# A hybrid decoder layer on one core: second feed-forward product by seven block products, first product in 256-wide parts

## The chip, the cores and the metric

The kernel runs on one core of a Trainium2 chip. The metric is the device time of one execution in microseconds (us). The kernel before takes 1446.87 us (median of 3 runs, 1446.61 to 1447.17).

## The reference

One layer on 256 tokens of width 2048, all in float32: a mixer (gated delta net and RWKV7 beside each other), a cross attention to 256 memory tokens, and a feed-forward part. The change touches the last:

```
h = h + squared_relu_mlp(rmsnorm(h, ffn_norm_w), ffn_w1, ffn_w2)   # max(u @ w1, 0)**2 @ w2
return rmsnorm(h, final_norm_w)
# w1: 2048 x 8192, w2: 8192 x 2048, both float32 and read once
```

## The kernel before

Engines are named as in the profile: PE is TensorE, DVE VectorE, ACT ScalarE, POOL GpSimd, SP the engine whose queue issues most transfers. The array multiplies in float32r, a shorter format, so every float32 operand x is split in two parts: hi is x rounded to float32r (a cast, on ACT), lo is x minus hi (a subtraction, on DVE). A product of two split operands takes three passes: hi hi, hi lo and lo hi. This holds for all large products; the weights are split as they arrive (`weights`, L228).

Stages, in the order of time: low-rank parts, RWKV7, delta net, output projection, cross attention, and from 721.9 us on the feed-forward, which is half of the span. It has four chunks (`ch`), and each chunk does two things.

First product, `gemm_T` (L261), four calls of four blocks each, 64 blocks in all. A block gives 128 hidden columns, transposed: [128 hidden, 256 tokens]. It has 16 k tiles. The weights are the stationary operand, and the moving operand holds x_hi and x_lo of a k tile beside each other, 512 columns. For each k tile L272 multiplies w_lo with x_hi (256 columns), and L273 multiplies w_hi with both halves (512 columns), into the two halves of one PSUM bank. `relu2` (L1186) then adds the halves (ACT copy, DVE add), squares the positive part (DVE) and splits it for the second product (ACT cast, DVE subtraction).

Second product, `gemm` (L244), four calls a chunk, one for each 512 of the 2048 output columns: 16 k tiles, two halves of the tokens, three passes of 512 columns each (L254 to L256), 96 matmuls a call and 1536 in all. The result is scaled and added to h by DVE. The very last call is `gemm_rows` (L205), which finishes the first 128 tokens before the others. Then `final` (L1140) applies the last norm and writes the output.

A block of weights of 512 KB comes from HBM by SP's queue into one of five buffers (pool `wp`, tag raw) and is split in pieces of [128 x 512]; three buffers each hold whi and wlo. The eight PSUM banks are three with the tag g (large products), two each of s0 and s1, and one x. The order on each engine is not the program's: a list scheduler places the instructions by priorities and its own estimate of times, and weight loads and splits have a high priority (`tc.high_priority(3000)`). Each engine then runs its own list in order, and waits on semaphores.

Of the kernel before, what the change touches and what calls it, by code (L numbers as in the profile page):

```python
# [17 lines left out]
P = 128  # L18
D = 2048
# [21 lines left out]
def host_layout(inp):  # L41
# [32 lines left out]
    def col(v):  # L74
# [22 lines left out]
        "w1": blocks_T(a["ffn_w1"][0]), "w2": blocks(a["ffn_w2"][0]),  # L97
# [7 lines left out]
def body(ctx, tc, I, out, dbg=None, upto=99):  # L105
# [65 lines left out]
    # derived per-channel scalars  # L171
# [15 lines left out]
    def lhs_split(raws, wname, pool, tag):  # L187
        """raw^T (times the norm's weight) split in two float32r parts, four k tiles a tile, as they are asked for."""
# [16 lines left out]
    def gemm_rows(lhs, wblk, evac, kbs, his, los):  # L205
        """the same, the first 128 tokens before the others, from weights that all stay."""
        kbs, w = list(kbs), []
        for m in range(2):
            acc = bank("g")
            for i, kb in enumerate(kbs):  # L210
                if m == 0:
                    with tc.high_priority(3000):
                        raw = wp.tile([P, KB, NB], F32, tag="raw", name=nm("raw"))
                        nc.sync.dma_start(out=raw, in_=wblk[kb])
                        hi, lo = his(), los()
                        A.copy(hi, raw)
                        tt(lo, raw, hi.bitcast(F32), ALU.subtract)
                    w.append((hi, lo))
                hi, lo = w[i]
                for q in range(KB):  # L220
                    first, last = i == 0 and q == 0, i == len(kbs) - 1 and q == KB - 1
                    xh, xo = lhs(kb * KB + q, m)
                    T.matmul(acc, lhsT=xh, rhs=hi[:, q], start=first, stop=False)
                    T.matmul(acc, lhsT=xh, rhs=lo[:, q], start=False, stop=False)
                    T.matmul(acc, lhsT=xo, rhs=hi[:, q], start=False, stop=last)  # L225
            evac(m, acc)

    def weights(src, a, b, parts):  # L228
        """a block of weights [128, a, b] in two float32r parts."""
# [14 lines left out]
    def gemm(lhs, wblk, n, evac, kbs=None):  # L244
        """[256 tok, n] = lhs^T @ W: three float32r products stand for the float32 one."""
# [15 lines left out]
    def gemm_T(rhs, wblk, evac):  # L261
        """(x W)^T in four parts of 128 columns, [128 col, (W x_hi, W_hi x_lo)]; rhs(kt) is (x_hi, x_lo)^T, 512 wide."""
        for j in range(4):
            acc = bank("g")
            for b in range(2):
                w = weights(wblk[j, b], 8, P, 2)
                for k in range(8):
                    first, last = b == 0 and k == 0, b == 1 and k == 7
                    x = rhs(8 * b + k)
                    xf = x.rearrange("p a t -> p (a t)")  # L270
                    if not first:
                        T.matmul(acc[:, 0:S], lhsT=w[k][1], rhs=x[:, 0], start=False, stop=False)  # L272
                    T.matmul(acc, lhsT=w[k][0], rhs=xf, start=first, stop=last)  # L273
                    if first:
                        T.matmul(acc[:, 0:S], lhsT=w[k][1], rhs=x[:, 0], start=False, stop=False)
            evac(j, acc)
# [84 lines left out]
    # the clock of the array rises and the functions' table loads while the first operands are on their way  # L361
# [73 lines left out]
    # gates of the deltanet: [tok, chunk, head]  # L435
# [35 lines left out]
    inv = [0]  # L471

    def inverse(B, pool, pool2):
        """B is overwritten with the inverse of I + (its strictly upper part); what lies below its diagonal is zero.

        X12 = -X11 B12 X22 for blocks of 2 to 128, the larger ones on tiles of the array."""
# [11 lines left out]
        def quarters(t, n):  # L488
            """the quarters 11, 12, 22 of the diagonal blocks of 2n: [q, block, row, column]."""
# [94 lines left out]
    def rw_shift(pt, c0, names, blks):  # L584
        """columns c0.. of the projection [tok, col] to shifted [col, tok] tiles of two blocks."""
# [12 lines left out]
    def rw_unit(u, r, k, v):  # L598
# [59 lines left out]
        # bonus * v  # L658
# [8 lines left out]
        # scores  # L667
# [21 lines left out]
        # [tok, .] forms  # L689
# [57 lines left out]
        # group norm, bonus, gate  # L747
# [94 lines left out]
    def dn_unit(g, kq, v2):  # L842
# [6 lines left out]
        # norms per token: [tok, (k/q), chunk, head]  # L849
# [21 lines left out]
        # decays, scores  # L871
# [72 lines left out]
        # norm over the head, times silu(z)  # L944
# [90 lines left out]
    def tok_T(src, wname):  # L1035
        """transposes of src [tok, 2048] (times the norm's weight), split in two parts, four k tiles a step."""
# [77 lines left out]
    rf = rms(h, "rf")  # L1114
    tt(rf, rf, rf, ALU.mult)
    mix.close()
    fp = ctx.enter_context(tc.tile_pool(name="fp", bufs=5, reuse_waits="tile"))
    fw = fp.tile([P, D], F32, name="fw", bufs=1)
    A.dma_start(out=fw, in_=I["fnw"].to_broadcast([P, D]))
    part = small.tile([P, 2, 8], F32, tag="sk", name=nm("ssp"))  # L1120

    def low():
        for _ in range(2):
            t = da.tile([P, 2, KB, NB], F32R, tag="kq", bufs=2, name=nm("llo"))
            yield t[:, 0]
            yield t[:, 1]
        for _ in range(4):
            yield fp.tile([P, KB, NB], F32R, tag="llo", bufs=4, name=nm("llo"))

    def high():  # L1130
        for _ in range(4):
            t = lx.tile([P, 2, KB, NB], F32R, tag="lx", name=nm("lhi"))
            yield t[:, 0]
            yield t[:, 1]

    llo, lhi = low(), high()

    def final(m):
        ss = part[:, m, 7:8]
        stt(ss, part[:, m, 4:5], 1.0 / D, part[:, m, 6:7], ALU.mult, ALU.add)  # L1140
        ro = small.tile([P, 1], F32, tag="ro", name=nm("ro"))
        power(ro, ss, -0.5, 1)
        for q in range(4):
            d = h[:, m, q * NB:(q + 1) * NB]
            if q == 3:
                stt(d, d, ro, fw[:, q * NB:], ALU.mult, ALU.mult)
            elif q:
                act(d, d, AF.Copy, scale=ro)
            else:
                ts(d, d, ro, ALU.mult)  # L1150
            (A if q % 2 else nc.sync).dma_start(out=out[m * P:(m + 1) * P, q * NB:(q + 1) * NB], in_=d)

    def add_ffn(gcol):
        def f(m, p):
            d = h[:, m, gcol * NB:(gcol + 1) * NB]
            stt(d, p, rf[:, m:m + 1], d, ALU.mult, ALU.add)
        return f

    def last_h(gcol):
        def f(m, p):  # L1160
            sl = slice(gcol * NB, (gcol + 1) * NB)
            d = h[:, m, sl]
            stt(d, p, rf[:, m:m + 1], d, ALU.mult, ALU.add)
            rms_part(h, part, m, gcol)
            tt(d, d, fw[:, sl], ALU.mult)
        return f

    def last(m, p):
        """the last 512 columns in two halves, so that little is left to do once the second's sum of squares is there."""
        V.tensor_reduce(part[:, m, 5:6], part[:, m, 0:3], axis=AX.X, op=ALU.add)  # L1170
        ts(part[:, m, 5:6], part[:, m, 5:6], 1.0 / D, ALU.mult, EPS, ALU.add)
        for i in range(2):
            d = h[:, m, 3 * NB + i * S:3 * NB + (i + 1) * S]
# [51 lines left out]
```

## Time and profile before

| | |
|---|---|
| median of 3 runs | 1446.87 us |
| span of the profiled execution, first to last instruction | 1442.5 us |
| median less the span (start and end around it) | 4.4 us |
| feed-forward, 721.9 us to the last matmul | 712.5 us |
| last matmul to the end of the span | 8.1 us |
| PE, DVE, ACT busy over the span | 98%, 66%, 54% |

The page's parts give the busy time of each engine, the DMA engines over 40 slices of the span, the chain that ended last, and groups of equal instructions. A matmul row's length contains its way through the array; matmuls overlap, so the distance from one start to the next is what one costs, not its length. The same holds in a small way for DVE and ACT, where the next instruction starts a little before the end of the one ahead.

### The profile page before, as it was taken

The page shows a single profiled execution, that of the slowest core. Times are in us where ns is not written, and L with a number is a line of the kernel's source. Part 1 is how long each engine was busy: PE and PEld are TensorE (multiplying, and loading weights), DVE is VectorE, ACT ScalarE, POOL GpSimd, SP SyncE. Part 2 cuts the span into 40 slices and gives each one's busy share as a digit, 9 for nine tenths or more (in the row PEclk, how much of TensorE's full clock was granted, in tenths as well). Part 3 has the DMA queues.
Part 4 walks back from the last instruction along what each step waited for, and adds up shares of the span by engine and source line. Part 5 has one row for each costly group of instructions (what it writes and reads, how often), then busy time and mean ns, then how long its engine had stood idle before and what let it go on. Part 6 is the DMA issues. An engine that isn't in the chain of part 4 may idle for free.

```text
span 1442.5 us, 22496 instructions
## 1 busy us (share of the span) xinstructions
PE 1414.8 (98%) x8284; PEld 1168.9 (81%) x8284; DVE 950.1 (66%) x1799; ACT 780.8 (54%) x1491; POOL 50.6 (4%) x66
## 2 busy tenths in 40 slices
PE   9999999999999989999999999999999999999997
PEld 7877788787876868887788888888888888888886
DVE  7748574869587685767676655666556665566664
ACT  7656454555456454566565544555445554455553
POOL 0010001100010000000000000000000000000000
PEclk9999999999999999999999999999999999999999
DMA  7444433454366464556465556555665555655554
GB/s 281 157 145 152 135 121 112 147 177 144 102 200 207 138 190 146 166 173 212 136 209 186 190 192 197 185 187 189 193 197 186 185 190 194 195 182 187 191 188 146
DMA packets 90688, 252.88 MB, mean 175 GB/s; under 512 B 20673, under 2 KB 29393, under 8 KB 90193
## 3 DMA queue, kind: packets, MB, share of 16 engines
q1 hardware_dynamic: 70304, 243.96, 51.2%
q10 hardware_dynamic: 19920, 6.42, 1.8%
q8 instruction: 65, 1.06, 0.3%
q0 software_dynamic: 352, 1.06, 0.2%
q14 instruction: 47, 0.38, 0.1%
HBM read 244.72 MB, written 6.69 MB: 174 GB/s over the span
## 4 chain that ended last, share of the span: by engine, by line
PE 82%; DMA 7%; DVE 6%; ACT 3%; issue 2%; SPq 0%; POOL 0%; ACTq 0%; POOLq 0%; DVEq 0%
PE ps_g L273 16%; PE ps_g L255 16%; PE ps_g L254 15%; PE ps_g L256 15%; PE ps_g L272 8%; DVE wlo L110 2%; PE ps_s L675 2%; DMA scr<-Sc 1%; DMA xc<-inv 1%; DMA mraw<-in_memT_dram 1%; PE ps_x L312 1%; DMA g<-scr 1%; DVE xtmp L110 1%; DMA junk<-in_mem_dram 1%; PE ps_s L312 1%
## 5 line engine op out<-in xcount | busy, mean ns | idle before, releaser
L110 DVE TENSOR_TENSOR wlo<-raw,whi 128x512 fp32r<-128x512 f32 x848 | 583.3, 691 | 388.1 <-ACT whi L239 386.8
L239 ACT CAST whi<-raw 128x512 fp32r<-128x512 f32 x848 | 523.4, 621 | 489.8 <-DVE wlo L110 203.7
L273 PE MATMUL ps_g<-hhl,whi 128*128 128x512 f32 x1024 | 357.6, 398 | 0.2 <-ACT whi L239 0.2
L272 PE MATMUL ps_g<-hhl,wlo 128*128 128x256 f32 x960 | 269.9, 281 | 0.0
L273 PEld LDWEIGHTS ps_g<-hhl,whi 128*128 128x128 f32 x1024 | 188.4, 188 | 42.5 <-ACT whi L239 0.5
L255 PE MATMUL ps_g<-wlo,xhl 128*128 128x512 f32 x512 | 209.9, 410 | 8.4 <-DVE wlo L110 8.3
L256 PE MATMUL ps_g<-whi,xhl 128*128 128x512 f32 x512 | 202.0, 395 | 0.0
L256 PE MATMUL ps_g<-whi,flo 128*128 128x512 f32 x480 | 186.7, 389 | 0.0
L255 PE MATMUL ps_g<-wlo,fhi 128*128 128x512 f32 x480 | 186.7, 389 | 0.0
L254 PE MATMUL ps_g<-whi,xhl 128*128 128x512 f32 x512 | 180.8, 406 | 3.4 <-ACT whi L239 3.4
L272 PEld LDWEIGHTS ps_g<-hhl,wlo 128*128 128x128 f32 x960 | 181.5, 189 | 2.8 <-ACT hhl L122 0.2
L254 PE MATMUL ps_g<-whi,fhi 128*128 128x512 f32 x480 | 151.3, 389 | 0.0
L255 PEld LDWEIGHTS ps_g<-wlo,xhl 128*128 128x128 f32 x512 | 96.6, 189 | 37.7 <-DVE wlo L110 18.2
L254 PEld LDWEIGHTS ps_g<-whi,xhl 128*128 128x128 f32 x512 | 94.6, 189 | 26.7 <-ACT whi L239 5.9
L256 PEld LDWEIGHTS ps_g<-whi,xhl 128*128 128x128 f32 x512 | 96.7, 189 | 18.8 <-issue 0.7
L255 PEld LDWEIGHTS ps_g<-wlo,fhi 128*128 128x128 f32 x480 | 90.1, 188 | 18.8
L256 PEld LDWEIGHTS ps_g<-whi,flo 128*128 128x128 f32 x480 | 90.1, 188 | 18.7
L254 PEld LDWEIGHTS ps_g<-whi,fhi 128*128 128x128 f32 x480 | 90.1, 188 | 18.6
L113 DVE SCALAR_TENSOR_TENSOR cy<-ps_x,colt,cy 128x255 f32<-128x255 f32 (+2 forms) x72 | 34.2, 476 | 10.9 <-ACT cy L122 10.3
L1191 ACT CAST fhi<-hid 128x256 fp32r<-128x256 f32 x64 | 26.1, 408 | 9.5 <-DVE hid L113 0.8
L113 DVE SCALAR_TENSOR_TENSOR hid<-hid 128x256 f32<-128x256 f32 x64 | 27.2, 425 | 2.2
L113 DVE SCALAR_TENSOR_TENSOR h<-ps_g,rf,h 128x512 f32<-128x512 f32 (+1 forms) x34 | 22.8, 712 | 8.0 <-PE ps_g L225 8.0
(360 smaller groups left out, 1540.7 us busy)
## 6 DMA issues: line engine op xcount, KB each, us to landing
raw<-in_w_dram SPq DMA_DIRECT2D x256, 512.0 KB, 3.5
raw<-in_w_in_dram SPq DMA_DIRECT2D x112, 512.0 KB, 3.5
raw<-in_w_out_dram SPq DMA_DIRECT2D x32, 512.0 KB, 3.5
raw<-in_wk_dram SPq DMA_DIRECT2D x8, 512.0 KB, 3.5
mraw<-in_memT_dram SPq DMA_DIRECT2D x8, 512.0 KB, 3.6
raw<-in_wq_dram SPq DMA_DIRECT2D x8, 512.0 KB, 3.4
raw<-in_wv_dram SPq DMA_DIRECT2D x8, 512.0 KB, 3.7
raw<-in_wo_dram SPq DMA_DIRECT2D x8, 512.0 KB, 3.5
```

The lines of the kernel that those rows point to most:

```text
L110: return (e or V).tensor_tensor(o, a, b, op=op)
L113: return V.scalar_tensor_tensor(o, a, s, b, op0=op0, op1=op1)
L239: A.copy(hi, w)
L254: T.matmul(acc[m][:, :n], lhsT=xh, rhs=w[q][0], start=first, stop=False)
L255: T.matmul(acc[m][:, :n], lhsT=xh, rhs=w[q][1], start=False, stop=False)
L256: T.matmul(acc[m][:, :n], lhsT=xl, rhs=w[q][0], start=False, stop=last)
L272: T.matmul(acc[:, 0:S], lhsT=w[k][1], rhs=x[:, 0], start=False, stop=False)
L273: T.matmul(acc, lhsT=w[k][0], rhs=xf, start=first, stop=last)
L312: T.transpose(out=o[:, j * P:(j + 1) * P], in_=a, identity=ident)
L675: T.matmul(bb[hl][:, 256 * i:256 * i + 256], lhsT=BK[hs, j, i, cs], rhs=AR[hs, j, :, cs], start=True, stop=True)
L1191: A.copy(hi[:, j], t)
```

## The change

Second product. The matrix product of 2 x 2 blocks is formed from seven block products instead of eight (Strassen's scheme in Winograd's form). The token halves and pairs of k tiles make the left blocks A11, A12, A21, A22; the weights of the same pairs of k tiles and of two groups of 512 columns make the right blocks. Left sums S1 to S4 come from POOL subtractions (`lefts`, 64 of [128 x 256]), are split by ACT and DVE, and are made once for 512 hidden columns. Right sums are made for each `quad` (two k tiles by 1024 columns; 64 quads). `rights` loads three blocks (rawq, 768 KB) and a pair of blocks (t13, 512 KB) on SP's queue, and then POOL issues a transfer that adds another pair of blocks, 512 KB from HBM, onto t13 in SBUF. Two DVE additions of [128 x 512] make the other pair of sums (t24). All seven right blocks are split: three pieces (bs, bt, bu) of 1536, 1024 and 1024 columns, each with a single buffer. The seven products go to seven PSUM banks (g, g, g, s0, s0, s1, s1) and are summed there over 4 or 8 quads (nine visits to an output half); then `add_products` adds them to h, with 11 DVE instructions of [128 x 512] and one ACT copy a visit.

First product. A k tile takes three matmuls of 256 columns into one half of a bank: w_hi with x_hi, w_hi with x_lo, w_lo with x_hi. Of eight k tiles all w_hi come before all w_lo. `relu2` is one ACT relu out of PSUM and one DVE square. After the first eight blocks the bank is x, of which there is one.

Order of the program: eight blocks of the first product, then for each of the 64 quads the quad and, as long as there are any, one more block. So 56 quads have a block beside them and the last eight do not. `gemm_rows` is gone; the final norm is spread over the last two visits.

```diff
+    def quads(w):
+        b = w.reshape(w.shape[0] // 512, 2, 2, P, w.shape[1] // 1024, 2, NB)
+        b = b.transpose(0, 2, 4, 3, 1, 5, 6).reshape(-1, 2, w.shape[1] // 1024, P, 4, NB)
+        return np.ascontiguousarray(b[:, :, :, :, [0, 1, 3, 2, 0]])
...
-                for k in range(8):
-                    first, last = b == 0 and k == 0, b == 1 and k == 7
-                    x = rhs(8 * b + k)
-                    xf = x.rearrange("p a t -> p (a t)")
-                    if not first:
-                        T.matmul(acc[:, 0:S], lhsT=w[k][1], rhs=x[:, 0], start=False, stop=False)
-                    T.matmul(acc, lhsT=w[k][0], rhs=xf, start=first, stop=last)
...
+                for part in range(2):
+                    for k in range(8):
+                        x = rhs(8 * b + k)
+                        first, last = b == 0 and k == 0 and part == 0, b == 1 and k == 7 and part == 1
+                        T.matmul(acc[:, 0:S], lhsT=w[k][part], rhs=x[:, 0], start=first, stop=last)
+                        if part == 0:
+                            T.matmul(acc[:, 0:S], lhsT=w[k][0], rhs=x[:, 1], start=False, stop=False)
...
+    def lefts(g, base):
+
+        sm_ = fp.tile([P, 4, 2, P], F32, tag="sm", name=nm("sm"))
+        tt(sm_[:, 0], base[:, 0], base[:, 2], ALU.subtract, e=G)
+        tt(sm_[:, 1], base[:, 1], sm_[:, 0], ALU.subtract, e=G)
+        tt(sm_[:, 2], base[:, 0], base[:, 1], ALU.subtract, e=G)
+        tt(sm_[:, 3], base[:, 3], sm_[:, 1], ALU.subtract, e=G)
...
+    def rights(src):
+
+        with tc.high_priority(3000):
+            raw = da.tile([P, 3, NB], F32, tag="kq", bufs=2, name=nm("rawq"))
+            nc.sync.dma_start(out=raw, in_=src[:, 2:5])
+            t13 = wp.tile([P, 2, NB], F32, tag="raw", name=nm("t13"))
+            nc.sync.dma_start(out=t13, in_=src[:, 0:2])
+            G.dma_start(out=t13, in_=src[:, 1:3], accum_op=ALU.add)
+            t24 = wp.tile([P, 2, NB], F32, tag="raw", name=nm("t24"))
+            tt(t24[:, 0], raw[:, 0], t13[:, 0], ALU.add)
+            tt(t24[:, 1], raw[:, 1], t24[:, 0], ALU.add)
+            b22, b21, b11 = split(raw, 3, "bs")
+            t1, t3 = split(t13, 2, "bt")
+            t2, t4 = split(t24, 2, "bu")
...
+    def quad(g, q, p, acc, first, last, order, done):
+        r = rights(I["w2"][g, q, p])
+        hi, lo = left[g]
+        for n in order:
+            xh, xl_ = hi[:, LHS[n], q], lo[:, LHS[n], q]
+            T.matmul(acc[n], lhsT=xh, rhs=r[n][0], start=first, stop=False)
+            T.matmul(acc[n], lhsT=xh, rhs=r[n][1], start=False, stop=False)
+            T.matmul(acc[n], lhsT=xl_, rhs=r[n][0], start=False, stop=last)
+            if last:
+                done(n)
...
+    jblock(8)
...
+        for g in gs:
+            for q in range(2):
+                end = g == gs[-1] and q == 1
+                order = (1, 2, 3, 5, 6, 7, 4) if end else (1, 2, 3, 5, 7, 6, 4)
+                quad(g, q, p, acc, g == gs[0] and q == 0, end, order, done)
+                jblock()
```

How the instructions stand. In the rows below the number behind a name is that of its buffer, so that rows of one quad or block can be told apart. DVE in the second chunk's first product, before: per block four subtractions wlo and three instructions of relu2.

```order
L110 TENSOR_TENSOR wlo_9736<-raw_9733,whi_9735 128x512
L110 TENSOR_TENSOR wlo_9740<-raw_9733,whi_9739 128x512
L110 TENSOR_TENSOR wlo_9762<-raw_9759,whi_9761 128x512
L110 TENSOR_TENSOR hid_9726<-ps_g_9673,hid_9726 128x256
L113 SCALAR_TENSOR_TENSOR hid_9726<-hid_9726 128x256
L110 TENSOR_TENSOR wlo_9766<-raw_9759,whi_9765 128x512
L110 TENSOR_TENSOR flo_9672<-hid_9726,fhi_9671 128x256
```

DVE at the same stage of the change, one quad and one block (t, bs, bt, bu belong to quads, wlo and base to blocks; rawq_10121 is the quad after rawq_10008):

```order
L116 TENSOR_TENSOR bs_10130<-rawq_10121,bs_10129 128x1536
L116 TENSOR_TENSOR t_2046_10013<-rawq_10008,t_2045_10010 128x512
L116 TENSOR_TENSOR bt_10021<-t_2045_10010,bt_10020 128x1024
L116 TENSOR_TENSOR wlo_9968<-raw_9961,whi_9967 128x512
L116 TENSOR_TENSOR t_2046_10013<-rawq_10008,t_2046_10013 128x512
L116 TENSOR_TENSOR wlo_10054<-raw_10051,whi_10053 128x512
L116 TENSOR_TENSOR wlo_10058<-raw_10051,whi_10057 128x512
L116 TENSOR_TENSOR bu_10025<-t_2046_10013,bu_10024 128x1024
L116 TENSOR_TENSOR wlo_10088<-raw_10085,whi_10087 128x512
L116 TENSOR_TENSOR base_9589<-base_9589 128x2x128
```

Ten instructions, 6912 columns, stand where seven with 2816 stood; the first addition t reads t_2045, which the adding transfer fills, and it stands ahead of the block's subtractions.

DVE's last rows before:

```order
L113 SCALAR_TENSOR_TENSOR h<-ps_g_14160,rf,h 128x256 x2
L113 SCALAR_TENSOR_TENSOR ssp_7522<-ssp_7522 128x1 x2
L117 TENSOR_SCALAR h<-h,ro_14219 128x512
L113 SCALAR_TENSOR_TENSOR h<-h,ro_14219,fw 128x512
```

And in the change, from the second to last product (ps_s_2982) on; ps_s_2980 is the last one:

```order
L116 TENSOR_TENSOR u_15086<-ps_s_2982_14914,u_15062 128x512
L119 SCALAR_TENSOR_TENSOR h<-u_15086,rf,h 128x512
L116 TENSOR_TENSOR u_15105<-ps_s_2983_14915,u_15086 128x512
L119 SCALAR_TENSOR_TENSOR ssp_7522<-ssp_7522 128x1
L119 SCALAR_TENSOR_TENSOR h<-u_15105,rf,h 128x512
L119 SCALAR_TENSOR_TENSOR h<-u_15105,nrf,h 128x512
L119 SCALAR_TENSOR_TENSOR h<-h,ro_15092,fw 128x512
L123 TENSOR_SCALAR h<-h,ro_15092 128x512
L119 SCALAR_TENSOR_TENSOR h<-ps_s_2980_14912,rf,h 128x512
L116 TENSOR_TENSOR h<-h,fw 128x512
```

Eight instructions stand between the end of the second to last product and the addition of the last.

## Rows read from the trace of the kernel before

**Rows 1.** The page: busy time by engine, and the chain that ended last.

```profile
PE 1414.8 (98%) x8284; PEld 1168.9 (81%) x8284; DVE 950.1 (66%) x1799; ACT 780.8 (54%) x1491; POOL 50.6 (4%) x66
...
PE 82%; DMA 7%; DVE 6%; ACT 3%; issue 2%; SPq 0%; POOL 0%; ACTq 0%; POOLq 0%; DVEq 0%
```

**Rows 2.** Stretches: us, busy by engine (instructions), granted clock, DMA share, GB/s.

```profile
721.90:1434.40 712.50, 712.24 (x3597) 603.62 (x3596) 445.19 (x754) 370.47 (x665) 1.25 (x2) 1.00 0.57 189
...
901.90:992.30 90.40, 90.40 (x514) 78.50 (x513) 60.86 (x112) 49.89 (x94) 0.00 (x0) 1.00 0.57 187
992.30:1079.30 87.00, 87.00 (x385) 72.04 (x384) 48.92 (x74) 40.60 (x66) 0.00 (x0) 1.00 0.60 193
...
1434.40:1442.50 8.10, 0.00 (x0) 0.00 (x0) 2.33 (x6) 2.24 (x6) 0.56 (x1) 0.71 0.36 129
```

**Rows 3.** Timeline of PE, first product: start, length, instruction.

```profile
902.15 0.28 PE L275 MATMUL ps_g<-hhl,wlo 128*128 128x256 f32 x1
902.26 0.28 PE L272 MATMUL ps_g<-hhl,wlo 128*128 128x256 f32 x1
```

**Rows 4.** Timeline of PE, low-rank parts, first and last of seven matmuls in a row.

```profile
12.83 0.29 PE L403 MATMUL ps_s<-wlo,xhl 128*128 128x272 f32 x1
...
13.59 0.29 PE L404 MATMUL ps_s<-whi,xhl 128*128 128x272 f32 x1
```

**Rows 5.** Groups by form, 721.9 to 1434.4: busy us, mean ns, idle before.

```profile
L110 DVE TENSOR_TENSOR wlo<-raw,whi 128x512 fp32r<-128x512 f32 x495 | 342.2, 692 | 250.3 <-ACT whi L239 250.2
L239 ACT CAST whi<-raw 128x512 fp32r<-128x512 f32 x495 | 307.7, 622 | 315.1 <-DVE wlo L110 178.5 <-PE ps_g L273 106.2 <-PE ps_g L256 29.5
...
L110 DVE TENSOR_TENSOR flo<-hid,fhi 128x256 fp32r<-128x256 f32 x64 | 26.9, 420 | 0.0
...
L113 DVE SCALAR_TENSOR_TENSOR h<-ps_g,rf,h 128x512 f32<-128x512 f32 x30 | 21.0, 743 | 0.0
...
L110 DVE TENSOR_TENSOR llo<-raw,lhi 128x1024 fp32r<-128x1024 f32 x8 | 9.7, 1223 | 4.4 <-ACT lhi L216 4.4
L216 ACT CAST lhi<-raw 128x1024 fp32r<-128x1024 f32 x8 | 8.4, 1050 | 5.5 <-DMA raw<-in_w_dram 5.5
```

**Rows 6.** Timeline of DVE, one instruction right behind another.

```profile
908.42 0.69 DVE L110 TENSOR_TENSOR wlo<-raw,whi 128x512 fp32r<-128x512 f32 x1 [0.73 <-ACT whi L239]
909.03 0.42 DVE L110 TENSOR_TENSOR hid<-ps_g,hid 128x256 f32<-128x256 f32 x1
```

**Rows 7.** Waits, 721.9 to 1434.4: us in total, times, longest.

```profile
DVE wlo L110 <- ACT whi L239: 250.2, 395, 1.0
```

**Rows 8.** Timeline, delta net: a POOL instruction and DVE's beside it.

```profile
419.50 0.64 POOL L880 TENSOR_SCALAR_AFFINE_SELECT Dm<-Dm 128x512 f32<-128x512 f32 x1 [1.01 <-ACT Dm L122]
419.68 1.00 DVE L110 TENSOR_TENSOR wlo<-raw,whi 128x512 fp32r<-128x512 f32 x1
```

**Rows 9.** The page: DMA share in 40 slices (tenths), GB/s, and one issue.

```profile
DMA  7444433454366464556465556555665555655554
GB/s 281 157 145 152 135 121 112 147 177 144 102 200 207 138 190 146 166 173 212 136 209 186 190 192 197 185 187 189 193 197 186 185 190 194 195 182 187 191 188 146
...
raw<-in_w_dram SPq DMA_DIRECT2D x256, 512.0 KB, 3.5
```

**Rows 10.** Groups on POOL, whole span: a DMA issue.

```profile
L575 POOL DMA_DIRECT2D o_dram<-y x4 | 3.1, 768 | 29.6 <-DVE cy L113 15.0 <-PE ps_g L256 8.3 <-ACT whi L239 6.3
```

**Rows 11.** Timeline behind the last matmul.

```profile
1434.39 0.88 DVE L113 SCALAR_TENSOR_TENSOR h<-ps_g,rf,h 128x256 f32<-128x256 f32 x2 [7.50 <-PE ps_g L225]
...
1436.67 1.33 ACT L122 ACTIVATE h<-h,ro 128x512 f32<-128x512 f32 x2 [0.86 <-POOL ro L110]
```

More of the change, by code (lines that the diff above doesn't have):

```diff
@@ L203, in lhs_split @@
         return get
[L205 to L226, printed above, removed]
     def weights(src, a, b, parts):
@@ L1115, in body @@
     tt(rf, rf, rf, ALU.mult)
+    nrf = const.tile([P, 2], F32, name="nrf")
+    ts(nrf, rf, -1.0, ALU.mult)
     mix.close()
-    fp = ctx.enter_context(tc.tile_pool(name="fp", bufs=5, reuse_waits="tile"))
-    fw = fp.tile([P, D], F32, name="fw", bufs=1)
-    A.dma_start(out=fw, in_=I["fnw"].to_broadcast([P, D]))
+    fp = ctx.enter_context(tc.tile_pool(name="fp", bufs=1, reuse_waits="tile"))
     part = small.tile([P, 2, 8], F32, tag="sk", name=nm("ssp"))
[L1122 to L1140, printed above, removed]
+    A11, A22, A12, S1, S2, S3, S4 = range(7)
+    left = {}
+    def relu2(base):
+        def f(j, p):
+            t = p[:, 0:S].rearrange("p (a t) -> p a t", a=2)
+            d = base[:, 2 * (j // 2):2 * (j // 2) + 2, j % 2]
+            act(d, t, AF.Relu)
+            tt(d, d, d, ALU.mult)
+        return f
@@ new lines, in split @@
+    def split(src, n, tag):
+        hi = fp.tile([P, n, NB], F32R, tag=tag + "h", name=nm(tag))
+        lo = fp.tile([P, n, NB], F32R, tag=tag + "l", name=nm(tag))
+        A.copy(hi, src)
+        tt(lo, src, hi.bitcast(F32), ALU.subtract)
+        return [(hi[:, i], lo[:, i]) for i in range(n)]
+    def rights(src):
[11 more added lines that the diff above has]
+            t2, t4 = split(t24, 2, "bu")
+        return {1: b11, 2: b21, 3: b22, 4: t4, 5: t1, 6: t2, 7: t3}
@@ new lines, in add_products, with add, tmp, both @@
+    def add_products(p, acc, after=None):
+        def add(m, c, x, by=rf):
+            d = h[:, m, 1024 * p + NB * c:1024 * p + NB * (c + 1)]
+            stt(d, x, by[:, m:m + 1], d, ALU.mult, ALU.add)
+        u = {}
+        def tmp(n):
+            u[n] = ptp.tile([P, NB], F32, tag="pt", name=nm("u"))
+            return u[n]
+        def both():
+            if 6 in u and 7 in have and 8 not in u:
+                tt(tmp(8), acc[7], u[6], ALU.add)
+                add(0, 1, u[8])
+                if after:
+                    after(0, 1)
+                add(0, 0, u[8], nrf)
+        have = set()
+        def done(n):
+            have.add(n)
+            if n == 1:
+                A.copy(tmp(1), acc[1])
+                add(1, 0, acc[1])
+            elif n == 2:
+                add(1, 0, acc[2])
+                if after:
+                    after(1, 0)
+            elif n == 3:
+                add(1, 1, acc[3])
+            elif n == 5:
+                add(1, 1, acc[5])
+                add(0, 1, acc[5])
+            elif n == 6:
+                tt(tmp(6), acc[6], u[1], ALU.subtract)
+                add(1, 1, u[6])
+                if after:
+                    after(1, 1)
+                both()
+            elif n == 7:
+                both()
+            elif n == 4:
+                add(0, 0, acc[4])
+                if after:
+                    after(0, 0)
+        return done
@@ new lines, in body, with square_sum @@
+    visits = []
+    for i in range(8):
+        for p in ((0, 1) if i % 2 == 0 else (1, 0)):
+            if visits and visits[-1][0] == p:
+                visits[-1][1].extend((2 * i, 2 * i + 1))
+            else:
+                visits.append((p, [2 * i, 2 * i + 1]))
+    fw = fp.tile([P, D], F32, name="fw")
+    def square_sum(m, c, slot):
+        junk = ptp.tile([P, NB], F32, tag="pt", name=nm("junk"))
+        act(junk, h[:, m, c * NB:(c + 1) * NB], AF.Square, accum=part[:, m, slot:slot + 1])
@@ L1153, in add_ffn @@
[L1153 to L1173, printed above, removed]
-            stt(d, p[:, i * S:(i + 1) * S], rf[:, m:m + 1], d, ALU.mult, ALU.add)
-            junk = ptp.tile([P, S], F32, tag="pt", name=nm("junk"))
-            act(junk, d, AF.Square, accum=part[:, m, 3 + i:4 + i])
-        stt(part[:, m, 6:7], part[:, m, 3:4], 1.0 / D, part[:, m, 5:6], ALU.mult, ALU.add)
-        final(m)
@@ new lines, in after_last, with jblock @@
+            (A if k % 2 else nc.sync).dma_start(out=out[m * P:(m + 1) * P, q * NB:(q + 1) * NB], in_=d)
+    bases = {}
+    nj = [0]
+    def jblock(n=1):
+        for _ in range(n):
+            if nj[0] == 64:
+                return
+            g, j = divmod(nj[0], 4)
+            if j == 0:
+                bases[g] = da.tile([P, 4, 2, P], F32, tag="v2", name=nm("base"))
+            gemm_T(hl, I["w1"][g], relu2(bases[g]), js=(j,), tag="g" if nj[0] < 8 else "x")
+            if j == 3:
+                lefts(g, bases[g])
+            nj[0] += 1
@@ new lines, in body @@
+    jblock(8)
+    A.dma_start(out=fw, in_=I["fnw"].to_broadcast([P, D]))
+    for v, (p, gs) in enumerate(visits):
+        acc = [None] + [bank(t) for t in ("g", "g", "g", "s0", "s0", "s1", "s1")]
+        after = {len(visits) - 1: after_last, len(visits) - 2: lambda m, c: early(m, 2 + c, c)}.get(v)
+        done = add_products(p, acc, after)
+        for g in gs:
[4 more added lines that the diff above has]
+                jblock()
```

67 lines of the change are left out of this document (31 added, 36 removed).

## The prediction

> **What bounds the kernel now.** I read the busy times first: PE is busy for 98% of the span, DVE for 66%, ACT for 54%, and the chain that ended last is PE for 82% [rows 1]. A busy share mixes stages, so I went to the stretches next. In the feed-forward, the only stage that the change touches, PE is busy for 712.24 of 712.5 us at the full clock (1.00), DVE for 445, ACT for 370, POOL for 1.3 [rows 2]. PE never waits there, so the stage is worth what its matmuls cost, and every other engine has room: DVE 37%, ACT 48%. The waits say the same: DVE waits 395 times for ACT's cast, 0.63 us each [rows 7], because it has nothing else to do. So the change takes work from PE and gives work to DVE, ACT, POOL and the transfers, and the question is whether the room is enough.
>
> **What one instruction costs.** PE: a stretch of the second product takes 87.0 us for its 384 matmuls of 512 columns, 0.2266 us each; a stretch of the first product 90.4 us for 16 blocks, 5.65 us a block or 0.353 us for a pair of 256 and 512 columns [rows 2]. A 256 right behind a 256 starts 0.11 us later [rows 3]. Seven matmuls of 272 columns with changing stationary operands have a distance of 0.76 / 6 = 0.127 [rows 4]; less 16 columns at 0.2266 / 512 that is 0.120 for 256. So a 256 among others of 256 costs 0.11 to 0.12; I take 0.116.
> DVE: an instruction of 512 columns takes 0.692 us, one of 1024 takes 1.223 [rows 5], so a column costs 1.04 ns and 1536 columns 1.75. One right behind another starts 0.61 us after it though it lasts 0.69 [rows 6]: 0.08 is saved each time DVE does not wait. Back to back, then: 0.34 for 256 (0.42 less 0.08), 0.61 for 512, 0.88 for 768, 1.14 for 1024, 1.67 for 1536, and 0.66 for a scaled addition to h (0.743) [rows 5].
>
> **The change part by part.** *PE.* A block takes 48 matmuls of 256 columns: 48 x 0.116 = 5.57 us instead of 5.65 (5.3 to 5.8 by the two ends). A quad takes 21 of 512: 21 x 0.2266 = 4.76 us; 64 quads 304.6 instead of 1536 x 0.2266 = 348.1. PE alone would need 64 x 5.57 + 304.6 = 661 us instead of 712.5.
> *DVE.* A quad takes 1.67 + 2 x 1.14 for the three subtractions and 2 x 0.61 for the two sums, 5.17 us; before, its four blocks took 4 x 0.61 = 2.4. A block takes 4 x 0.61 for its weights, 0.34 for the square, and (0.88 + 1.14) / 4 for the left sums: 3.29. A visit adds nine scaled additions and two sums out of PSUM, 9 x 0.66 + 2 x 0.61 = 7.16. In all 64 x 8.46 + 9 x 7.16 = 606 us: where DVE had a third to spare it is now at 92% of PE's 661.
> *ACT.* 0.622 for 512 and 1.05 for 1024 [rows 5] make 1.48 for 1536 and 0.41 for 256: a quad 1.48 + 2.10, a block 4 x 0.62 + 0.41 + (0.84 + 1.05) / 4, some 6.9 us together beside PE's 10.3. Hidden.
> *Transfers.* A quad and a block bring eleven pieces of 256 KB (four, three, two, and two added): 2.88 MB in 10.4 us is 277 GB/s, after 189 at a share of 0.57 [rows 2]. By that row the 16 engines would carry 332 GB/s, by the first slice (281 GB/s at 7 tenths) 400 [rows 9]. So the share is 0.69 to 0.83 if an addition costs a plain transfer, and I take that it stays hidden. No row shows an adding transfer; from below it costs the same as a plain one, from above four of them (17 pieces, 4.46 MB), 11.1 to 13.4 us a period. Row and rule: plain loads of 512 KB land in 3.5 us [rows 9]. The Trainium skill (Collectives: The Full Stack, section "The bandwidth ceiling: the fold count and why AG ≠ RS ≠ AR") says that an add in the DMA path costs no cycles but reads two sources, which halves its rate; by that the two added pieces count four, 3.41 MB or 8.5 to 10.3 us a period, just under PE's, which no run here shows yet.
> *Latency.* t13 passes a load (3.5), POOL's issue (0.77) [rows 10] and a second load, at least 3.5, and then cast and subtraction (2.2): 10 us. Its buffer is the one that the second weight tile of the block two back left, some 13 us ahead. It fits with 3 us to spare. If it is late, DVE stands at the first sum t, and behind it in DVE's list stand bt and the next block's wlo, for which PE waits.
> *POOL and DVE.* POOL makes 64 subtractions from SBUF beside a full DVE. One row shows what may happen: while POOL's 0.64 us ran, a DVE subtraction took 1.00 instead of 0.69 [rows 8]. I price a meeting at 0 to 0.31 us, one a quad. The Trainium skill (SBUF — State Buffer, section "Who interferes with whom") states the rule: a DVE instruction with two SBUF inputs and a POOL instruction that reads SBUF share one read port, and the second to issue waits. Row and rule agree; by the rule each meeting costs, 64 x 0.31 = 20 us of DVE.
>
> **The sum, by phases.** First eight blocks: PE, 8 x 5.57 = 44.6 us (DVE needs 26).
> 56 periods of a quad and a block: PE 5.57 + 4.76 = 10.33. DVE back to back 8.46 and seven of the nine visits (7 x 7.16 / 56 = 0.90): 9.36; if all its 12 instructions wait and lose the 0.08, 10.3, and with a meeting 10.6. The ends lie close together, so I take a period of 10.5: 588 us.
> Last eight quads, with no block to fill PE: PE 38.1, but DVE 8 x 5.17 + 2 x 7.16 + 6 x 0.6 for the norm = 59, of which some 3 are done ahead: 56, by DVE. bs has one buffer, read by nine matmuls (2.04), cast (1.48) and subtracted (1.67): 5.2 a quad, the same bound. Between 41 (PE, if DVE runs far ahead) and 67.
> End: before, scaling began 2.3 us after the last matmul [rows 11] and the span ended after 8.1 [rows 2]. Now eight DVE instructions (4.4 us by their lengths above) stand ahead of the last product's addition, begun 0.45 us earlier: +4, so 12.1 us.
> 44.6 + 588 + 56 + 12.1 = 700.7 instead of 712.5 + 8.1 = 720.6: 19.9 us less. The span is 1442.5, so 1422.6; the median of the runs lies 4.4 above the span, so **1427 us**. PE's saving of 51 us shrinks to 20 because DVE takes the bound in the last quads (18) and nearly takes it in the periods (9).
>
> **The rivals.**
> A, PE keeps the bound throughout: periods of 10.33 (578.5), last quads 45, end 10. 678 us, 42 less, 1404. For it: every cover has 30% or more in the profile before, and the list of DVE holds splits a quad ahead. Against it: 9.36 of 10.33 is 91% for an engine that runs in order, more than any stretch here shows.
> B, DVE waits (slower): the added transfer is late, or a cast, and DVE's first sum holds up the block's weights. DVE's 10.6 plus one wait of the usual 0.63 [rows 7] a period is 11.25: 630 us; with 60 in the last quads and 12.1, 747, 26 more, 1473. It decides from a period of (720.6 - 44.6 - 56 - 12.1) / 56 = 10.86, only 0.36 above my own. For it: single buffers for bs, bt, bu, a chain of two transfers with 3 us to spare. Against: before, the same list scheduler left PE waiting for 0.3 us in 712.
> C, the transfers bind: an addition costs four plain ones, 13.4 us a period: 750 + 44.6 + 56 + 12.1 = 863, 142 more, 1589; at 11.1 us 14 more, 1461. Against: the share was 0.57, and 281 GB/s did run at 7 tenths.
> D, no change: a period of 10.8 to 10.9, both shares of the gain spent.
> That the first product's three 256s cost more than the pair they replace: at 0.120 a block is 5.76, 64 x 0.11 = 7 us more than before where PE binds; it lies inside the ranges.
>
> **Chances.** Forecast 0.35 (1414 to 1443), A 0.25, B 0.25, D 0.10, C 0.05. What a measurement of this kernel can tell from no change is about 0.2%, 2.9 us. A and the forecast are faster, 0.60; D is the same, 0.10; B and C are slower, 0.30. The range reaches over A and B and leaves out the ends of both and the worst of C: 1398 to 1480.
>
> **What would show it.** Right: in the feed-forward DVE busy for over 85%, PE's matmuls of 256 at 0.11 to 0.12, waits of PE for bs, bt, bu and wlo, most of them in the last eight quads; PE's idle there some 18 us. A shows in PE busy through all periods. B shows in DVE waiting at t for an added transfer, or at bs for ACT, with a period over 10.9 and PE's busy share below 95%. C shows in a DMA share near 1 and landings far above 3.5 us. The forecast is wrong if DVE has idle time and PE too: then a chain of single buffers binds, which I have priced only in the last quads.

## The result and the profile after

The changed kernel takes 1626.67 us (1621.22 to 1631.69) beside 1447.02 of the kernel before: a ratio of 1.124, 95% interval 1.120 to 1.128. The forecast was 1427, its range 1398 to 1480, and the upper bound of case C, 1589, lay nearest. The profiled span is 1624.6 us instead of 1442.5.

The page of the changed kernel, busy times and the chain that ended last, against [rows 1]; under them two lines of its DMA queues (packets, MB, share of 16 engines' span) and the issues of t13 (count, KB each, median us to landing):

```profile
PE 1462.5 (90%) x9116; PEld 1220.6 (75%) x9116; DVE 1137.3 (70%) x1839; ACT 835.7 (51%) x1408; POOL 173.6 (11%) x194
...
q1 hardware_dynamic: 70304, 260.74, 48.5%
q0 software_dynamic: 9568, 34.62, 12.0%
...
DMA 11%; DVE 5%; PE 3%; issue 3%; ACT 1%; POOL 0%; POOLq 0%; SPq 0%; DVEq 0%; ACTq 0%
...
t<-in_w_dram SPq DMA_DIRECT2D x64, 512.0 KB, 4.6
t<-in_w_dram POOLq DMA_DIRECT2D x64, 512.0 KB, 7.8
```

The shares of the chain are shares of the span, and here they add up to some 23%: it could be followed back only from the end to 1240 us. In that part DMA has the largest share, 11 of the 23 points, and PE 3, where PE had 82 of 100 before; no engine is full. The adding transfer lands 7.8 us after its issue, a plain one of the same size after 4.6. A stretch of the changed kernel, columns as in [rows 2]:

```profile
1000.00:1100.00 100.00, 84.11 (x490) 72.89 (x488) 69.33 (x86) 46.38 (x64) 11.90 (x12) 0.93 0.73 211
```

Where PE had been busy for all but 0.3 us of 712, it now lacks 16 us of 100, and DVE is at 69%, not at the 90% on which the forecast rested. PE and DVE are idle at once: the sign that the prediction named for a chain of single buffers. The granted clock of the stretch is 0.93, so some of PE's matmuls ran slower as well; what part of the loss that is, no run separates. Waits from 720 to 1625 (total us, times, longest), against [rows 7]:

```profile
ACT bt L1136 <- DMA t<-in_w_dram: 226.1, 48, 10.2
...
DVE t L116 <- DMA t<-in_w_dram: 170.9, 47, 7.7
...
PEld ps_s L1163 <- ACT bt L1136: 102.8, 44, 5.0
```

In 47 or 48 of the 64 quads ACT and DVE wait for the adding transfer, and 44 times PE waits for ACT's cast of what it brought. SP waits too; L1146 is the load of a t13, L1144 that of a rawq:

```profile
SPq L1144 <- DVE t L116: 255.8, 58, 10.9
SPq L1146 <- DVE wlo L116: 204.5, 46, 11.2
```

In 46 of 64 cases, then, what the load waited for last was a subtraction of DVE from a weight tile; the loads of rawq waited for the sums t. One turn, from the timelines of SP, POOL and DVE (start, length, instruction, and in brackets the idle time before it):

```profile
1117.40 0.33 SPq L1146 DMA_DIRECT2D t<-in_w_dram  x1
...
1122.45 0.88 POOL L1147 DMA_DIRECT2D t<-in_w_dram  x1 [12.52 <-DVE wlo L116]
...
1131.43 0.69 DVE L116 TENSOR_TENSOR t<-rawq,t 128x512 f32<-128x512 f32 x1 [2.95 <-DMA t<-in_w_dram]
1132.04 0.68 DVE L116 TENSOR_TENSOR wlo<-raw,whi 128x512 fp32r<-128x512 f32 x1
...
1132.75 0.33 SPq L1146 DMA_DIRECT2D t<-in_w_dram  x1
```

Read it as a ring. SP issues the first load of a t13 at 1117.40; POOL issues the adding transfer at 1122.45; as soon as that has landed DVE makes the first sum t, at 1131.43; behind t in DVE's list stands wlo, which ends at 1132.72, and 0.03 us later SP issues the load of the *next* t13, into the buffer that this wlo had read. The turn took 15.35 us. Over quads 2 to 55 the loads of t13 follow each other by 13.64 us on the mean; from one load's issue to the landing of its addition are 13.0 us. In 33 of 53 turns the next load is issued only after t has begun, and these turns take 15.0 us from one t to the next; in the other 20 it is issued earlier, mostly behind a wlo that stands ahead of t, and they take 11.5. Of the 13.0 us the first load takes 4.7 on the mean, then 0.7 pass to POOL's issue, and the addition lands 7.6 after the start of that issue.

By the phases of the prediction (first block to the end of the eighth, with its relu; 56 periods; rest):

| kernel | first blocks | 56 periods | one period | last quads and end |
|---|---|---|---|---|
| forecast | 44.6 | 588 | 10.5 | 68.1 |
| changed kernel | 54.5 | 771.8 | 13.78 | 79.0 |
| g2, one quad's blocks kept | 53.7 | 600.8 | 10.73 | 44.7 |
| f3, own buffers, plain transfer | 54.1 | 618.2 | 11.04 | 69.8 |
| e3, own buffers for t13 | 54.5 | 628.2 | 11.22 | 76.9 |

Of the 202 us by which the changed kernel misses the forecast, 184 are in the periods. The first phase misses by 9 in g2 too, which has no supply to wait for: its PE stands still for a few us only, but a block takes 5.76 us and not 5.57 (f1), and matmuls of other parts fall into it, 12 of the first quad's 21 among them, which I had counted to the periods.

### The profile page after: what moved, and what is told of

It reads as the page before. It is cut to its first block, busy times and chain, and to the rows that moved or that the text cites. A ratio compares the mean times of both kernels' runs of the same rounds, so it can differ in the third digit from the quotient of the medians.

```text
span 1624.6 us, 24242 instructions
## 1 busy us (share of the span) xinstructions
PE 1462.5 (90%) x9116; PEld 1220.6 (75%) x9116; DVE 1137.3 (70%) x1839; ACT 835.7 (51%) x1408; POOL 173.6 (11%) x194
## 3 DMA queue, kind: packets, MB, share of 16 engines
q0 software_dynamic: 9568, 34.62, 12.0%
## 5 line engine op out<-in xcount | busy, mean ns | idle before, releaser
L116 DVE TENSOR_TENSOR wlo<-raw,whi 128x512 fp32r<-128x512 f32 x608 | 414.3, 694 | 169.2 <-ACT whi L222 142.2
L222 ACT CAST whi<-raw 128x512 fp32r<-128x512 f32 x608 | 366.5, 618 | 246.6 <-PE ps_g L239 139.9
L254 PE MATMUL ps_x<-hhl,whi 128*128 128x256 f32 x896 | 224.7, 286 | 7.1 <-ACT whi L222 4.8
L256 PE MATMUL ps_x<-hhl,whi 128*128 128x256 f32 x896 | 224.0, 285 | 0.0
L116 DVE TENSOR_TENSOR t<-rawq,t 128x512 f32<-128x512 f32 x128 | 88.5, 691 | 171.1 <-DMA t<-in_w_dram 170.9
L254 PEld LDWEIGHTS ps_x<-hhl,whi 128*128 128x128 f32 x896 | 173.2, 193 | 14.0 <-ACT whi L222 6.1
L256 PEld LDWEIGHTS ps_x<-hhl,whi 128*128 128x128 f32 x896 | 173.3, 193 | 4.2
L254 PE MATMUL ps_x<-hhl,wlo 128*128 128x256 f32 x896 | 141.9, 291 | 11.2 <-DVE wlo L116 11.2
L116 DVE TENSOR_TENSOR bs<-rawq,bs 128x1536 fp32r<-128x1536 f32 x64 | 113.0, 1766 | 49.9 <-ACT bs L1136 49.7
L1136 ACT CAST bs<-rawq 128x1536 fp32r<-128x1536 f32 x64 | 94.3, 1474 | 104.0 <-DMA rawq<-in_w_dram 81.2
L254 PEld LDWEIGHTS ps_x<-hhl,wlo 128*128 128x128 f32 x896 | 131.0, 199 | 21.2 <-DVE wlo L116 13.2
L1164 PE MATMUL ps_g<-bs,ahi 128*128 128x512 f32 x192 | 87.1, 454 | 2.6 <-DVE bs L116 2.3
```

What stands on the lines that cost most here:

```text
L116: return (e or V).tensor_tensor(o, a, b, op=op)
L222: A.copy(hi, w)
L254: T.matmul(acc[:, 0:S], lhsT=w[k][part], rhs=x[:, 0], start=first, stop=last)
L256: T.matmul(acc[:, 0:S], lhsT=w[k][0], rhs=x[:, 1], start=False, stop=False)
L1136: A.copy(hi, src)
L1164: T.matmul(acc[n], lhsT=xh, rhs=r[n][1], start=False, stop=False)
```

## The experiments

The kernel before, run again beside the three sets of experiments, took 1444 to 1449 us. A ratio is estimated from all runs of its set, with a 95% interval; it is not the quotient of the two medians. The part ahead of the feed-forward, which no edit touches, took 719 to 731 us in the profiled runs, so a difference of a few us between two versions says little.

**e1: no adding transfer.** The rest of the program is as in the changed kernel; the list scheduler orders it anew.

```
-            G.dma_start(out=t13, in_=src[:, 1:3], accum_op=ALU.add)
```

> Leaves the adding transfer out (t13 keeps one pair of blocks, the other is never added). Loop theory: a quad's pair t13 passes load (4.6 us to land), 0.6, POOL's issue 0.87 and the adding transfer (6.9 from issue), and the next quad's load waits for a weight subtraction that stands behind the first sum in DVE's list, so the period is 13.6 us; without the adding transfer the loop loses 8.4 us, falls to some 5 to 6, and PE or DVE bind: period 10.3 to 10.8, 1425 to 1455 us. DVE theory (too much work on DVE, whatever the transfers do): little is gained, over 1560 us.

Measured: one run, 1482.6 us (span 1480.9), 28 above the loop theory's range and 77 below the rival's. The second transfer and its addition cost 144 us, with DVE's work as in the changed kernel: DVE's work is not what that time went for. Some 28 us more than the loop were left to find. A shorter ring is still in the trace: in 53 of 53 turns the next load is issued after t, 4.2 us on the mean, and the loads follow each other by 11.3 us, not by 10.3 to 10.8.

**e2: the second transfer plain.**

```
-            G.dma_start(out=t13, in_=src[:, 1:3], accum_op=ALU.add)
+            G.dma_start(out=t13, in_=src[:, 1:3])
```

> The second transfer onto t13 stays on POOL's queue and moves the same bytes, but overwrites instead of adding (the sums are left out). It keeps the chain of two transfers and its loop and takes away only what adding costs. Loop theory with an adding price: landing falls from 7.8 us to 4.5 to 5, the period from 13.6 to some 10.8 to 11.5, 1460 to 1510 us. Capacity of the chain alone (adding costs nothing beyond a plain transfer): 1600 us or more. POOL-queue theory (issue held up behind its subtractions): no change, over 1600 us.

Measured: one run, 1514.3 us (span 1512.5), 4 above the first range: 112 less than with the addition and 32 more than without the transfer. From the issue of the load to the landing of the second transfer there are 10.6 us on the mean instead of 13.0, and the loads of t13 follow each other by 11.8 us instead of 13.6. 2.4 us less in the chain are 1.8 us less in the period: the period follows the chain. This is the cleanest of the comparisons, since the instructions of the feed-forward stand in the same order on every engine as in the changed kernel; only the clock differs beside the transfer (0.99 from 1000 to 1400, and 0.94 in the changed kernel).

**e3: t13 in two buffers of its own.** The memory comes from the last norm's weights, which move into four small tiles. Two things more change with it: only three tiles a period instead of four share the ring of five, and the list scheduler puts the instructions in another order on every engine.

```
-            t13 = wp.tile([P, 2, NB], F32, tag="raw", name=nm("t13"))
+            t13 = fp.tile([P, 2, NB], F32, tag="t13", bufs=2, name=nm("t13"))
...
-    fw = fp.tile([P, D], F32, name="fw")
+    fw = [da.tile([P, NB], F32, tag=("cy", "ct")[i % 2], bufs=2, name=nm("fw")) for i in range(4)]
```

> t13 gets two buffers of its own (the final norm's weights move to four tiles left over from the delta net), the adding transfer stays. Loop theory: the load of quad n+1 no longer waits for DVE's list behind quad n, the loop spans two quads (16 us for two, 8 a quad), and the next bound decides: DVE or PE at 10.5 us, or the 16 transfer engines, which by the packets of the changed kernel need 8.4 to 9.9 us a period; 1430 to 1480 us. Capacity theory (adding transfers bind by themselves): it stays above 1560 us. POOL-queue theory: above 1560 us too.

Measured: 1490.99 us (1487.24 to 1506.33), ratio to before 1.0325 [1.0261, 1.0389]: 136 us of the 180 are gone, but it is 11 above the range. That lies in the early periods (8 to 24 take 201 us, 12.6 each) and in the last quads (table). The chain of a t13 is no shorter (13.6 us on the mean), but the next load is now issued 5.6 us before the first sum, and after it in only 2 of 53 turns: two chains run side by side. How much of the 136 us is t13's buffer, how much the room in the ring and how much the new order, no run separates. A stretch of e3 from the middle of the feed-forward, columns as above:

```profile
1000.00:1400.00 400.00, 399.60 (x2598) 364.09 (x2597) 369.03 (x448) 249.63 (x324) 88.29 (x75) 1.00 0.89 270
```

PE is full, at the full clock, with DVE at 92% and DMA at 0.89: eight periods take 84.4 us, 10.55 each. That is the forecast's period of 10.5, though by PE and not by DVE. The buffers of bs, bt and bu are single here too, so it was not they that held the changed kernel at 13.6.

**e4: the sums for t13 on DVE from one plain load of four blocks.**

```
-            raw = da.tile([P, 3, NB], F32, tag="kq", bufs=2, name=nm("rawq"))
-            nc.sync.dma_start(out=raw, in_=src[:, 2:5])
+            raw = da.tile([P, 4, NB], F32, tag="kq", bufs=2, name=nm("rawq"))
+            nc.sync.dma_start(out=raw, in_=src)
...
-            nc.sync.dma_start(out=t13, in_=src[:, 0:2])
-            G.dma_start(out=t13, in_=src[:, 1:3], accum_op=ALU.add)
+            tt(t13, raw[:, 1:4:2], raw[:, 0:1].to_broadcast([P, 2, NB]), ALU.add)
```

> No adding transfer: one plain transfer of 1 MB brings the four blocks of a quad, and one more DVE addition of 1024 columns makes t13 (same result as the change). Loop theory: the chain of two transfers is gone and DVE binds: 606 + 64 x 1.14 = 679 us of DVE against 661 of PE, a period of 10.5 (back to back) to 11.8 (every instruction waits once, POOL's meetings), 1440 to 1490 us. Theory that DVE load was the cause: slower than the change, above 1630 us.

Measured: 1492.87 us (1492.77 to 1496.7), ratio 1.0309 [1.0279, 1.0339]; a miss by 3 us above the bound. The same stretch of e4:

```profile
1000.00:1400.00 400.00, 389.48 (x2485) 345.57 (x2484) 392.35 (x464) 234.96 (x310) 105.42 (x36) 1.00 0.55 188
```

Here DVE is the bound, 98% busy, at a period of 11.1. One more instruction of 1.21 us than in the changed kernel fills it, so the forecast's sum of DVE's work (9.4 to 10.6 a period) was right: e3's 369 us in 400 are 9.7 a period; in the changed kernel it just was not what ended last.

**f1: the first product alone.** The kernel before with the new first product.

```
-                    T.matmul(acc, lhsT=w[k][0], rhs=xf, start=first, stop=last)
+                        T.matmul(acc[:, 0:S], lhsT=w[k][part], rhs=x[:, 0], start=first, stop=last)
+                        if part == 0:
+                            T.matmul(acc[:, 0:S], lhsT=w[k][0], rhs=x[:, 1], start=False, stop=False)
```

> The kernel before with one part of the change alone: the first product as 48 matmuls of 256 a block (and the square out of PSUM by ACT's ReLU and one DVE product); the second product is the old one. By the distance of 0.120 us between matmuls of 256 that the changed kernel's trace shows, a block costs 5.76 instead of 5.65 us: 64 x 0.11 = 7 us more, 1452 to 1457. By the 0.116 that I had taken: 5.57, 5 us less, 1442. If it is over 1465, the first product alone explains a part of the loss that I have put down to the second.

Measured: 1454.78 us (1451.65 to 1459.29), ratio 1.0051 [1.0028, 1.0074]: 7.4 us, or 64 x 0.115, as the first expectation has it. Two neighbours on f1's timeline of PE, against [rows 3]:

```profile
736.56 0.28 PE L271 MATMUL ps_g<-hhl,whi 128*128 128x256 f32 x1
736.68 0.28 PE L273 MATMUL ps_g<-hhl,whi 128*128 128x256 f32 x1
```

They stand 0.12 us apart: the upper end of my 0.11 to 0.12.

**f2: e3 with the left-hand subtractions on DVE.**

```
-        tt(sm_[:, 0], base[:, 0], base[:, 2], ALU.subtract, e=G)
+        tt(sm_[:, 0], base[:, 0], base[:, 2], ALU.subtract)
...
```

> e3 (t13 in two buffers of its own) with the four left-hand subtractions of a group on DVE instead of POOL, so that POOL's list holds only the adding transfers. Theory, POOL's list: the early periods of e3 (800 to 950 us, some 28 us lost) are late because an adding transfer stands in POOL's list behind a subtraction that waits for the group's base; with those gone they fall to 11 us a period, and the whole to 1460 to 1475. Rival, DVE: 16 x 4 x 0.34 = 22 us more DVE work, less the meetings (64 x 0.22 = 14 us); the steady stretch is PE's at 10.55 either way, and the time stays within 1485 to 1500.

Measured: 1500.17 us (1488.47 to 1503.86), ratio 1.0321 [1.0262, 1.0381], as e3. Both theories are half right. Periods 8 to 24 fall from 201 to 182 us, which speaks for POOL's list there; but the next 32 rise from 338 to 365, with losses at the group changes.

**f3: e3 with the second transfer plain.** The edit of e2 on e3.

> e3 with the second transfer into t13 plain instead of adding (t1 and t3 are not the sums that the reference needs: the addition is left out). If the loop through t13's buffer was what the adding transfer cost, the steady periods stay at 10.55 (PE's bound) and the time stays within 10 us of e3's 1491: 1481 to 1495. If the adding packets (328 ns instead of 159) also hold up the other loads at the start and in the last quads, 1455 to 1475.

Measured: 1466.98 us (1464.44 to 1471.34), ratio 1.0123 [1.0086, 1.0160]: between the two expectations, 24 us below e3, whose order on every engine it shares. The steady periods stay at 10.6 (8 of them in the middle take 84 us in both), so that loop is cut; what the adding packets still cost lies in the early periods and in the last quads (table: 10 and 7 us). The two lines of f3's queues for comparison:

```profile
q1 hardware_dynamic: 70304, 260.74, 53.1%
q0 software_dynamic: 9568, 34.62, 7.0%
```

The same packets take 7.0% of 1466.9 us here and 12.0% of 1624.6 us with the addition.

**f4: the sum for t13 on POOL.** e4 with one word more.

```
-            tt(t13, raw[:, 1:4:2], raw[:, 0:1].to_broadcast([P, 2, NB]), ALU.add)
+            tt(t13, raw[:, 1:4:2], raw[:, 0:1].to_broadcast([P, 2, NB]), ALU.add, e=G)
```

> e4 with the sum for t13 on POOL instead of DVE: four blocks in one plain 1 MB load, no second transfer. DVE loses 1.14 us a period (97 to 98 % busy in e4's steady stretch at 11.1 us) and meets a POOL instruction of some 3 us or more once a period. If a meeting costs DVE what it cost the four subtractions (0.22 to 0.3 us), the steady period falls to PE's 10.55 and the time to 1460 to 1475; if POOL's long sum holds DVE's two-input instructions for its whole length, it is 1500 or more.

Measured: one run, 1551.0 us (span 1549.3), 58 above e4. One meeting, from f4's timelines of POOL and of DVE:

```profile
1104.93 2.52 POOL L116 TENSOR_TENSOR t<-rawq 128x1024 f32<-128x1024 f32 x1 [11.84 <-DVE bt L116]
...
1104.77 0.42 DVE L116 TENSOR_TENSOR base<-base 128x256 f32<-128x256 f32 x1
1105.11 3.43 DVE L116 TENSOR_TENSOR bu<-t,bu 128x1024 fp32r<-128x1024 f32 x1
1108.46 1.82 DVE L116 TENSOR_TENSOR wlo<-raw,whi 128x512 fp32r<-128x512 f32 x2
```

bu, 1.22 us when alone, takes 3.43: what is left of POOL's 2.52 us, and then its own length. On the mean of all quads bu takes 2.04 us here and 1.27 in e4. Work moved from DVE to POOL came back to DVE as standing time.

**g1: e3 with both ends eased.**

```
+        by = V if g < 4 or g == 15 else G
...
+            t13 = (wp.tile([P, 2, NB], F32, tag="raw", name=nm("t13")) if nq[0] > 57 and nq[0] % 2 else
+                   fp.tile([P, 2, NB], F32, tag="t13", bufs=2, name=nm("t13")))
```

> e3 with two further edits at its ends: the left-hand subtractions of the first four groups and of the last one on DVE (POOL's list there holds adding transfers alone), and in the last seven quads every second t13 in the weights' ring of five, which is idle by then. Theory, ends: f2 brought the periods 8 to 24 from 201 to 182 us with the same edit and f3's last quads took 70 us instead of e3's 77, so this falls by 15 to 26, to 1465 to 1476. Rival: the early lateness is the adding packets' own (f3 gained 24 us by plain ones, with POOL's list as in e3), and the ends stay: 1485 to 1495.

Measured: 1480.46 us (1469.56 to 1484.47), ratio 1.0212 [1.0161, 1.0263], where e3 had 1.0325 [1.0261, 1.0389]. Between the expectations, and the two intervals touch, so its gain is not settled. In the profiled run periods 8 to 24 took 186 us instead of e3's 201 and the last part 74.4 instead of 76.9; three later group changes lost some 12 us together, which e3 had not.

**g2: one quad's right-hand blocks for all.** PE's matmuls stay, in an order that the scheduler made anew; 63 of 64 supplies go.

```
-        r = rights(I["w2"][g, q, p])
+        r = kept[0] if kept else rights(I["w2"][g, q, p])
+        kept[:] = [r]
```

> The changed kernel with the right-hand blocks of the first quad kept and used for all 64 quads: the other 63 quads load, add, cast and subtract nothing (so the second product is not the reference's). PE's list and the visits are as in the changed kernel. If all that the change lost against PE's own need lies in the supply of the quads, PE needs 64 x 5.76 + 64 x 4.76 = 673 us instead of 712.5, the end some 6 us more: 1410 to 1425 (the case that I had called A). If the group change (base, POOL's subtractions, alo) or the visits' additions make PE wait as well, 1430 to 1460; over 1480, the first product's supply is the bound.

Measured: 1423.93 us (1419.6 to 1428.93), ratio 0.9848 [0.9815, 0.9881], in the first expectation's upper end. The chain of waits of g2:

```profile
PE 83%; DMA 7%; DVE 6%; ACT 2%; issue 2%; SPq 0%; POOL 0%; POOLq 0%; ACTq 0%; DVEq 0%
```

PE holds the chain as in [rows 1]. Seven products instead of eight do save PE's time, and what the changed kernel loses comes with the supply of the quads.

**What the runs add up to.** From the 1447 of before: PE's own saving, with the dearer first product in it, brings 1424 (g2). Supplying the quads by plain transfers with own buffers for t13 makes it 1467 (f3, +43). Adding packets in place of plain ones: 1491 (e3, +24). t13 in the shared ring: 1627 (+136). The last two are not independent: in the shared ring the addition costs 112 (e2 to the changed kernel), since there most of what the chain gains is lost in the period. The last step also holds the new order that came with e3's buffers. No version here that does the whole computation beats the kernel before.

## Why the prediction was wrong

**The step that failed** is the one on latency: "Its buffer is the one that the second weight tile of the block two back left, some 13 us ahead. It fits with 3 us to spare." The tile is the right one, but the 13 us are no slack. It leaves its buffer when DVE has subtracted from it, and in DVE's list of the turn above that subtraction stands behind the first sum of the quad before. So the load of one t13 was issued 0.3 us before the t of the quad before on the mean, and up to its own t it had one period and those 0.3 us: at the forecast's 10.5 that is 10.8 us, and to the landing of its addition it needed 13.0. The prediction saw the pieces ("DVE stands at the first sum t, and behind it in DVE's list stand bt and the next block's wlo"), but took them for what a late transfer would do to PE. They also decide when the next transfer starts: a late t makes the next load late, and the period grows to the chain's length, 13.6 us. The turns of the changed kernel show it among themselves (15.0 us where the load came after t, 11.5 where it came before), and e2 shows it by the transfer alone. e3 removes the loop, but not by the buffer alone; a version with wlo and t exchanged was not run.

**The chain's length** was too short as well. To the landing of the addition I had counted 7.8 us (3.5, 0.77 and 3.5); it takes 13.0: 4.7 for the first load, 0.7 until POOL's issue, 7.6 from there to the landing, POOL's 0.87 included. The 3.5 of [rows 9] were a load's on engines at a share of 0.57; here, at 0.73, it was longer. Even at a plain transfer's price the chain was 10.6 us and the time 1514 (e2), above the range.

**Adding taken as a plain transfer.** Per MB the profile gives 12.0% x 16 x 1624.6 / 34.62 = 90 us of an engine for the adding queue and 48 for the plain one, 1.9 times. The Trainium skill (Collectives: The Full Stack, section "The bandwidth ceiling: the fold count and why AG ≠ RS ≠ AR") states, of the reduce step of a collective, that its add needs two source reads and so runs at half a copy's rate; the trace agrees in the packets' time, and half the rate would have been the better term. The landing grew by less, from 5.3 us (e2) to 7.8. Without the ring the term was worth 24 us (e3 against f3); in the ring it was worth 112.

**Case B** had the mechanism's name, "the added transfer is late", and a price of one usual wait of 0.63 us a period. That price came from a row on another wait [rows 7]; the waits for the addition were 10.2 us at the longest and 4.7 on the mean for ACT. It ought to have been the chain's length. That PE waited so little before spoke for little: the weights of that feed-forward come by plain loads, and none is issued onto what another has just brought. Case C's 1589 lay nearest by its number alone: the DMA share was 0.73 and not near 1.

**Right:** DVE's work (e4 fills it with one instruction more); ACT hidden; the engines' rate for plain transfers (277 GB/s forecast at a share of 0.69 to 0.83, f3 has 269 at 0.79); PE's saving as such, 1404 in case A and 1424 in g2, of which the 256s at 0.120 instead of 0.116 explain some 12 by the changed kernel's two block prices (64 x 0.19). PE's bound in the periods, not DVE's, holds in e3, where PE is busy for 399.6 of 400 us.

**Luck** is that the last quads and the end, 68.1 forecast, took 69.8 with plain transfers. The forecast has DVE full there; in f3 neither DVE nor PE is:

```profile
1397.00:1453.00 56.00, 38.92 (x125) 26.26 (x126) 44.39 (x52) 23.58 (x30) 4.93 (x7) 0.83 0.38 126
```

**Meetings of POOL and DVE,** priced at up to 0.31 us, were not separated for the short subtractions: moved to DVE they brought nothing in all (f2). The Trainium skill (SBUF — State Buffer, section "Who interferes with whom") has DVE and POOL wait for each other's whole instruction at a shared port; f4's meeting agrees, 3.43 us for 1.22, beside a POOL instruction of 2.52; the row that the prediction took its price from [rows 8] had one of 0.64.

## What to carry to other kernels

Before a chain of two transfers is called hidden, find the instruction that frees its buffer and see what stands ahead of that instruction in its engine's list: if it is a consumer of the same chain, the period can grow to the chain's whole length, here 13.6 us for a chain of 13.0, with the engines idle. The sign in a profile is that the bound engine and the full one are idle at once while a load is issued again and again right behind an instruction that waited for the load before. Here two buffers of its own, with the new order that came with them, brought 136 of 180 us back. Take a new kind of transfer at the price of its worst reading before its latency is counted as slack.

## What the runs showed of the hardware

- An adding transfer of 512 KB landed 7.8 us after its issue (changed kernel) or 7.2 (e3), a plain one on the same queue 5.3 (e2) or 5.2 (f3); the same packets took 12.0% of 1624.6 us of the 16 engines' time when they added and 7.0% of 1466.9 (f3) when not.
- POOL's issue of the adding transfer took 871 ns, of the plain one 552 (f3).
- Where PE waited in every period, the granted clock of the stretch was 0.93 on the mean (1000 to 1100), so a part of it ran at the lower of the two levels (1.2 and 2.4 GHz); in e3, where PE did not wait, it was 1.00, the upper level throughout (1000 to 1400).
- POOL's sum of 1024 columns took 3.09 us on the mean (f4, 950 to 1400), DVE's of the same size 1.21 (e4).
